# Opening of a hybrid encoder layer: first tokens loaded through two queues, and part of their normalization on ScalarE

## The chip, the cores and the metric

The kernel runs on one core of one Trainium2 chip. A core has five engines that work beside each other, each through its own list of instructions in order: TensorE (PE; PEld is its loading of stationary operands), VectorE (DVE), ScalarE (ACT), GpSimd (POOL) and SyncE (SP), which here only starts transfers (DMAs). Sixteen DMA engines move the data between the chip's memory and the core's SBUF. An engine waits for another through semaphores. The metric is the device time of one execution in microseconds (us); less is better.

## The reference, cut to what matters

```python
def layer_norm(x, g, b):
    mu = jnp.mean(xf, axis=-1, keepdims=True)
    var = jnp.mean(jnp.square(xf - mu), axis=-1, keepdims=True)
    return (xf - mu) * lax.rsqrt(var + LN_EPS) * g + b

def reference(x, emb_ln_g, emb_ln_b, w_in, conv_w, sink, w_out, ln_g, ln_b):
    h = layer_norm(x, emb_ln_g, emb_ln_b)          # x: 1 x 256 x 4096, float32
    p = h @ w_in[0]                                # 4096 x 13312
    ...                                            # gated convolution, windowed attention
    y = concat([y_conv, y_attn]) @ w_out[0]        # 4096 x 4096
    return layer_norm(2 ** 0.25 * h + y, ln_g[0], ln_b[0])
```

There are 256 tokens of 4096 features. Nearly all the work is in the two matrix products; the change lies wholly in the first `layer_norm` and in how its input comes in.

## The kernel before, in words

Every weight piece (128 x 2048 float32, 1 MB) is split into a high part in a rounded 32-bit format and the low remainder: ScalarE writes the high part (`split_hi`, L226, `whi`), VectorE the low one (`split_lo`, L230, `wlo`). Activations are split the same way into `xT` (`x_split`, L409 and L410). TensorE multiplies high by high, high by low and low by high (`mm`, L275; later in pairs of blocks at L300 to L303). The order of all engines is that of the code; no scheduler moves anything.

The opening deals with the 256 tokens in two halves of 128, `xs[0]` and `xs[1]`, with one token on each of 128 partitions. In turn:

- SP starts the transfers: `xs[0]` in six parts by columns (1024, 1024, 1024, 512, 256, 256), the scales `g_c` and `b_c`, the first weight piece `first[0]`, then `xs[1]` in four parts of 1024 columns with the halves of the weight piece `first[1]` between them, then the following weight pieces. Eight semaphores go round: each transfer waits until the one eight places earlier has landed.
- VectorE takes the statistics of `xs[0]` (`stats`, L354: nine instructions, seven over 512 columns and two over 256), combines them (`stats_end`, L357) and works out mean and 1/deviation in `musd` with one ScalarE instruction among four of its own (`small_chain`, L311 to L315; the ScalarE one is `y`). It then normalizes `xs[0]` in place in eight parts of 512 columns (`norm`, L362), takes the statistics of `xs[1]`, and normalizes that.
- TensorE first runs two matmuls without use, for warmth, as soon as columns 3072 to 3583 of `xs[0]` are there (L417). It turns the normalized parts (features onto partitions; `transp` L369 for parts 0 and 1, `transp2` L387 for the others), and ScalarE copies them out of PSUM into `hT` with the scale and bias of the layer norm (`turned1` L375, `turned2` L395).
- The products of the first two weight pieces are done in full float32 straight from `hT` (`first_mm`, L404): for the first tokens piece 0 and half of piece 1, then transposes of parts 2 and 3 of `xs[0]`, the rest of piece 1, and the same for the second tokens. From L275 on come the split weights, four rows of `hT` (a part) for each piece.

`musd[:, i, 2:3]` holds 1/deviation and `musd[:, i, 3:4]` holds minus mean times 1/deviation, so `x * musd[2] + musd[3]` is the normalized value too.

Of the kernel before, what the change touches and what calls it, by code (L numbers as in the profile page):

```python
# [8 lines left out]
F32 = mybir.dt.float32  # L9
F32R = mybir.dt.float32r  # L10
AF = mybir.ActivationFunctionType
# [3 lines left out]
P = 128  # L15
D = 4096
# [85 lines left out]
def encoder_kernel(ctx: ExitStack, tc: tile.TileContext, x, emb_g, emb_b, wi, ws, conv_w, sink, wo, ln_g, ln_b, out):  # L102
    nc = tc.nc
# [143 lines left out]
    musd = const.tile([P, 2, 4], F32, name="musd")  # L247
# [58 lines left out]
    def small_chain(i, dst):  # L306

        v = small.tile([P, 1], F32, name="v", bufs=1)
        y = small.tile([P, 1], F32, name="y0", bufs=1)
        t = small.tile([P, 1], F32, name="t", bufs=1)  # L310
        nc.scalar.activation(y, dst[:, i, 1:2], AF.Abs_reciprocal_sqrt, bias=eps_t)  # L311
        nc.vector.tensor_scalar(v, dst[:, i, 1:2], LN_EPS, -0.5, op0=ALU.add, op1=ALU.mult)
        nc.vector.scalar_tensor_tensor(t, y, v, y, op0=ALU.mult, op1=ALU.mult)
        nc.vector.scalar_tensor_tensor(dst[:, i, 2:3], t, 1.5, y, op0=ALU.add, op1=ALU.mult)
        nc.vector.scalar_tensor_tensor(dst[:, i, 3:4], dst[:, i, 0:1], -1.0, dst[:, i, 2:3], op0=ALU.mult, op1=ALU.mult)  # L315

    with tc.tile_pool(name="pro", bufs=1) as pro:
        warm = small.tile([P, 1], F32, name="sd", bufs=1)
        nc.scalar.activation(warm, eps_t, AF.Abs_reciprocal_sqrt)
        xs = [pro.tile([P, D], F32, name=f"x{i}") for i in range(2)]  # L320
        hT = pro.tile([P, KT, S], F32, name="hT")
        g_c = pro.tile([P, KT], F32, name="g_c")
        b_c = pro.tile([P, KT], F32, name="b_c")
# [1 line left out]
        def x_load(i, *cols):  # L325
            for c0, c1 in zip(cols, cols[1:]):
                nc.sync.dma_start(out=xs[i][:, c0:c1], in_=x[i * P:(i + 1) * P, c0:c1])
# [3 lines left out]
            nc.sync.dma_start(out=first[1][:, sl], in_=wi[IN_PIECES.index(steps[1][1:])][:, sl])  # L331

        first = [wpool.tile([P, PIECE + GAP], F32, name=f"first{j}", tag="whi")[:, OFF:OFF + PIECE] for j in range(2)]
        x_load(0, 0, 1024, 2048, 3072, 3584, 3840, 4096)
        nc.sync.dma_start(out=g_c, in_=emb_g)
        nc.sync.dma_start(out=b_c, in_=emb_b)
        load(0, first[0])
# [11 lines left out]
        NQ = KT // 4  # L349
# [6 lines left out]
        def stats_end(i):  # L356
            nc.vector.bn_aggr(musd[:, i, 0:2], st[i])  # L357
            small_chain(i, musd)

        def norm(i, q):  # L360
            sl = slice(q * 512, (q + 1) * 512)
            nc.vector.tensor_scalar(xs[i][:, sl], xs[i][:, sl], musd[:, i, 0:1], musd[:, i, 2:3],  # L362
                                    op0=ALU.subtract, op1=ALU.mult)

        def transp(i, q, pool, name):
            pt = pool.tile([P, 4, P], F32, name=name)
            for k in range(4):
                kt = q * 4 + k
                nc.tensor.transpose(pt[:, k, :], xs[i][:, kt * P:(kt + 1) * P], ident)  # L369
            return pt  # L370
# [30 lines left out]
        def first_mm(q, i, k0=0, k1=PK):  # L401
            for k in range(k0, k1):
                kt = q * PK + k
                nc.tensor.matmul(acc[0, i], hT[:, kt, i * P:(i + 1) * P], first[q][:, k * W:(k + 1) * W],  # L404
                                 start=(kt == 0), stop=False)
# [13 lines left out]
        for q in range(2):  # L419
            norm(0, q)  # L420
            t0.append(transp(0, q, ps_att, "att"))
# [1 line left out]
            turned1(0, q, t0[q])  # L423
        first_mm(0, 0)
        first_mm(1, 0, 0, 2)
        for q in range(2, NQ):
            norm(0, q)
        for c in range(NQ + 1):
            stats(1, c)
        transp2(2, (0,))  # L430
        transp2(3, (0,))
        first_mm(1, 0, 2, 4)
        stats_end(1)
        for q in range(NQ):
            norm(1, q)
        t1 = [transp(1, q, ps_acc, "acc") for q in range(2)]
# [398 lines left out]
    for j in range(n_pro, N_IN):  # L835
        kind, ci, q = steps[j]
# [332 lines left out]
```

## Time and profile before

| | |
|---|---|
| median of 3 runs | 1500.56 us (1500.46 to 1501.62) |
| the profiled execution | 1500.92 us, span 1499.2 us |
| TensorE busy | 1482.4 us (99%), granted clock 0.999 |
| VectorE busy | 1338.4 us (89%) |
| ScalarE busy | 803.3 us (54%) |
| DMA | 316.17 MB, mean 211 GB/s; 356 GB/s in the first 22 us |

All lines of the profile come from one execution. The span runs from its first instruction to its last, and the execution's own time is 1.7 us longer. Times in timelines count from the span's start. A row of a timeline gives the start, the length, the engine, the line of the code, the operation, its output and inputs, their shapes, how many instructions are merged in it, and in brackets how long the engine had been idle and what ended that. Buffers are named without their numbers: `x` is `xs[0]` or `xs[1]`, `first` is either of the first two weight pieces, `att` and `acc` are PSUM tiles, `st` the statistics.

### The profile page before, as it was taken

The numbers are of one execution on the slowest core, as the hardware profiler recorded it, in microseconds if no ns is written. First come the engines' busy times: TensorE is split into PE (matmuls) and PEld (weight loads), VectorE is DVE, ScalarE is ACT, GpSimd is POOL, SyncE is SP. The second block draws the span as 40 slices with busy tenths as digits, with TensorE's granted clock in tenths as the row PEclk, the third lists the DMA queues.
The fourth block names the chain that finished last, engine by engine and source line by source line (L and its number), as shares of the span: only waits on it lengthen the run. The fifth ranks groups of instructions, "written<-read, shape, count | busy, mean of one in ns | idle before, by whom it ended". The sixth has DMA issues, their size and how long they took to land.

```text
span 1499.2 us, 29810 instructions
## 1 busy us (share of the span) xinstructions
PE 1482.4 (99%) x12878; PEld 1465.4 (98%) x12878; DVE 1338.4 (89%) x1384; ACT 803.3 (54%) x687; POOL 1.3 (0%) x7
## 2 busy tenths in 40 slices
PE   7999999999999999999999999999999999999998
PEld 4999999999999999999999999999999999999997
DVE  7768999898999999999999999999998688888876
ACT  5544656766666665655555555555555444444431
POOL 0000000000000000000000000000000000000000
PEclk9999999999999999999999999999999999999999
DMA  8545465555554556646545655556558656756663
GB/s 318 217 183 196 164 217 189 192 197 208 180 204 176 190 201 209 230 177 224 200 182 219 231 198 197 225 204 241 191 207 313 233 201 220 290 215 230 219 237 113
DMA packets 71365, 316.17 MB, mean 211 GB/s; under 512 B 8545, under 2 KB 12609, under 8 KB 50113
## 3 DMA queue, kind: packets, MB, share of 16 engines
q1 hardware_dynamic: 70224, 312.43, 57.3%
q8 instruction: 101, 1.65, 0.4%
q10 hardware_dynamic: 1008, 1.84, 0.3%
q14 instruction: 32, 0.25, 0.0%
HBM read 305.23 MB, written 8.91 MB: 210 GB/s over the span
## 4 chain that ended last, share of the span: by engine, by line
PE 93%; DVE 3%; ACT 1%; issue 1%; DMA 1%; SPq 0%; ACTq 0%; DVEq 0%
PE acc L275 39%; PE acc L957 20%; PE pacc L301 6%; PE pacc L300 6%; PE pacc L303 6%; PE acc L301 4%; PE acc L300 4%; PE acc L303 4%; DVE wlo L230 1%; PE att L518 1%; ACT whi L226 1%; DVE st L354 0%; PE acc L404 0%; DMA wall<-in_ws 0%; DVE wall L192 0%
## 5 line engine op out<-in xcount | busy, mean ns | idle before, releaser
L226 ACT ACTIVATE whi<-wall 128x1792 fp32r<-128x1792 f32 (+1 forms) x284 | 501.7, 1772 | 464.6 <-DVE wall L194 149.7
L230 DVE TENSOR_TENSOR wlo<-wall,whi 128x1792 fp32r<-128x1792 f32 (+1 forms) x284 | 593.4, 2096 | 75.9 <-ACT whi L226 64.3
L275 PE MATMUL acc<-whi,xT 128*128 128x256 f32 x3584 | 427.6, 276 | 0.0
L275 PEld LDWEIGHTS acc<-whi,xT 128*128 128x128 f32 x3584 | 415.8, 188 | 0.0
L275 PE MATMUL acc<-wlo,xT 128*128 128x256 f32 x1792 | 221.3, 275 | 0.0
L275 PEld LDWEIGHTS acc<-wlo,xT 128*128 128x128 f32 x1792 | 211.4, 188 | 0.0
L226 ACT ACTIVATE whi<-w 128x2048 fp32r<-128x2048 f32 x73 | 140.7, 1927 | 114.6 <-PE acc L275 72.5
L957 PE MATMUL acc<-whi,xT 128*128 128x256 f32 x1696 | 201.8, 275 | 0.0
L957 PEld LDWEIGHTS acc<-whi,xT 128*128 128x128 f32 x1696 | 196.6, 188 | 0.4 <-issue 0.4
L230 DVE TENSOR_TENSOR wlo<-w,whi 128x2048 fp32r<-128x2048 f32 x73 | 166.8, 2286 | 10.8 <-ACT whi L226 10.6
L192 DVE TENSOR_TENSOR wall<-wall 128x1024 f32<-128x1024 f32 x93 | 113.3, 1218 | 11.0 <-DMA wall<-in_ws 8.7
L300 PE MATMUL acc<-whi,xT 128*128 128x256 f32 x416 | 114.7, 276 | 0.0
L301 PE MATMUL acc<-whi,xT 128*128 128x256 f32 x416 | 114.6, 276 | 0.0
L300 PE MATMUL pacc<-whi,xT 128*128 128x256 f32 x396 | 111.0, 280 | 0.0
L303 PE MATMUL pacc<-wlo,xT 128*128 128x256 f32 x396 | 109.2, 276 | 0.6 <-DVE wlo L230 0.4
L301 PE MATMUL pacc<-whi,xT 128*128 128x256 f32 x396 | 109.1, 276 | 0.0
L957 PE MATMUL acc<-wlo,xT 128*128 128x256 f32 x848 | 105.3, 275 | 0.0
L303 PE MATMUL acc<-wlo,xT 128*128 128x256 f32 x416 | 104.4, 275 | 0.0
L300 PE MATMUL pacc<-whi,SC 128*128 128x256 f32 x376 | 103.6, 275 | 0.0
L301 PE MATMUL pacc<-whi,SC 128*128 128x256 f32 x376 | 103.6, 275 | 0.0
L957 PEld LDWEIGHTS acc<-wlo,xT 128*128 128x128 f32 x848 | 100.4, 188 | 0.0
L303 PE MATMUL pacc<-wlo,SC 128*128 128x256 f32 x376 | 94.5, 276 | 0.0
(224 smaller groups left out, 1930.1 us busy)
## 6 DMA issues: line engine op xcount, KB each, us to landing
wall<-in_ws SPq DMA_DIRECT2D x202, 512.0 KB
w<-in_wi SPq DMA_DIRECT2D x73, 1024.0 KB
wall<-in_wo SPq DMA_DIRECT2D x43, 1024.0 KB
wall<-in_wi SPq DMA_DIRECT2D x39, 1024.0 KB
R<-in_wo SPq DMA_DIRECT2D x10, 1024.0 KB
x<-in_x SPq DMA_DIRECT2D x7, 512.0 KB
yl<-yd SPq DMA_DIRECT2D x7, 512.0 KB
xc<-in_x SPq DMA_DIRECT2D x14, 256.0 KB
```

Of the source, the lines that this page charges most:

```text
L192: nc.vector.tensor_tensor(t[:, :, 4:6, :], t[:, :, 1:3, :], t[:, :, 0:1, :].to_broadcast([P, 2, 2, HW]), op=ALU.add)
L226: nc.scalar.activation(part(j, wh[j]), part(j, raw[j]), AF.Copy)
L230: nc.vector.tensor_tensor(part(j, wl[j]), part(j, raw[j]), part(j, wh[j]).bitcast(F32), op=ALU.subtract)
L275: nc.tensor.matmul(acc[ci, i][:, c:c + HW], x, w[:, k * W + c:k * W + c + HW], start=(first and w is hi and k + off + c == 0), stop=(last ...
L300: nc.tensor.matmul(o, ah, hi[:, w, :], start=(opens and p == 0), stop=False)
L301: nc.tensor.matmul(o, al, hi[:, w, :], start=False, stop=False)
L303: nc.tensor.matmul(o, ah, lo[:, w, :], start=False, stop=(closes and last))
L518: nc.tensor.transpose(ps[:, c, i * P:(i + 1) * P], t[:, i, (2 * b + c) * P:(2 * b + c + 1) * P], ident)
L957: nc.tensor.matmul(acc[ci, i][:, c:c + HW], y, m[:, k * w + c:k * w + c + HW], start=(first and off + c == 0), stop=(last and c + HW == w))
```

## The change

The six transfers of `xs[0]` are written first. They are cut at other columns (512, 1024, 1024, 1024, 256, 256), and two of them, columns 0 to 511 and 1536 to 2559, are issued by ScalarE, ahead of its table load and its warming activation. Of the eight normalization parts of `xs[0]`, parts 0 and 1 stay on VectorE; parts 2 to 7 go to ScalarE as `Identity(scale * x + bias)` in the new `norm_act`. Parts 2 and 3 stand where all six stood; parts 4 to 7 stand behind the statistics of `xs[1]` (behind their `small_chain`) and ahead of the normalization of `xs[1]`.

```diff
     with tc.tile_pool(name="pro", bufs=1) as pro:
+        xs = [pro.tile([P, D], F32, name=f"x{i}") for i in range(2)]
+        for eng, c0, c1 in ((nc.scalar, 0, 512), (nc.sync, 512, 1536), (nc.scalar, 1536, 2560), (nc.sync, 2560, 3584),
+                            (nc.sync, 3584, 3840), (nc.sync, 3840, 4096)):
+            eng.dma_start(out=xs[0][:, c0:c1], in_=x[0:P, c0:c1])
         warm = small.tile([P, 1], F32, name="sd", bufs=1)
         nc.scalar.activation(warm, eps_t, AF.Abs_reciprocal_sqrt)
-        xs = [pro.tile([P, D], F32, name=f"x{i}") for i in range(2)]
...
-        x_load(0, 0, 1024, 2048, 3072, 3584, 3840, 4096)
...
+        def norm_act(q):
+            sl = slice(q * 512, (q + 1) * 512)
+            nc.scalar.activation(xs[0][:, sl], xs[0][:, sl], AF.Identity, scale=musd[:, 0, 2:3], bias=musd[:, 0, 3:4])
...
         first_mm(1, 0, 0, 2)
-        for q in range(2, NQ):
-            norm(0, q)
+        for q in range(2, 4):
+            norm_act(q)
         for c in range(NQ + 1):
             stats(1, c)
...
         stats_end(1)
+        for q in range(4, NQ):
+            norm_act(q)
         for q in range(NQ):
             norm(1, q)
```

What ScalarE has in its list from the start to the first split weight, before (`x_105` and `x_106` are the two halves of the tokens, `y_147` and `y_214` the ScalarE step of each half's statistics):

```order
L319 ACT_TABLE_LOAD
L319 ACTIVATE sd<-eps_t 128x1
L311 ACTIVATE y_147<-musd,eps_t 128x1
L375 ACTIVATE hT<-att,b_c,g_c 128x128 x8
L311 ACTIVATE y_214<-musd,eps_t 128x1
L375 ACTIVATE hT<-acc,b_c,g_c 128x128 x4
L226 ACTIVATE whi<-wall 128x2048
```

The same after the change (the first tokens are now `x_103`, the second step `y_210`; lines are a few numbers higher):

```order
L321 DMA x_103<-in_x 128x512
L321 DMA x_103<-in_x 128x1024
L323 ACT_TABLE_LOAD
L323 ACTIVATE sd<-eps_t 128x1
L311 ACTIVATE y_147<-musd,eps_t 128x1
L381 ACTIVATE hT<-att,b_c,g_c 128x128 x8
L369 ACTIVATE x_103<-x_103,musd 128x512 x2
L311 ACTIVATE y_210<-musd,eps_t 128x1
L369 ACTIVATE x_103<-x_103,musd 128x512 x4
L381 ACTIVATE hT<-acc,b_c,g_c 128x128 x4
L226 ACTIVATE whi<-wall 128x2048
```

Two transfers stand ahead of the table load, two parts ahead of the second `y`, and four between the second `y` and the first `hT` of the second tokens.

VectorE between the two statistics, before:

```order
L354 BN_STATS st_132<-x_105 128x6 x9
L357 BN_AGGR musd<-st_132 128x2
L312 TENSOR_SCALAR v<-musd 128x1
L313 SCALAR_TENSOR_TENSOR t<-y_147,v 128x1
L314 SCALAR_TENSOR_TENSOR musd<-t,y_147 128x1
L315 SCALAR_TENSOR_TENSOR musd<-musd 128x1
L362 TENSOR_SCALAR x_105<-x_105,musd 128x512 x8
L354 BN_STATS st_133<-x_106 128x6 x9
```

And after:

```order
L356 BN_STATS st_132<-x_103 128x6 x9
L359 BN_AGGR musd<-st_132 128x2
L312 TENSOR_SCALAR v<-musd 128x1
L313 SCALAR_TENSOR_TENSOR t<-y_147,v 128x1
L314 SCALAR_TENSOR_TENSOR musd<-t,y_147 128x1
L315 SCALAR_TENSOR_TENSOR musd<-musd 128x1
L364 TENSOR_SCALAR x_103<-x_103,musd 128x512 x2
L356 BN_STATS st_133<-x_104 128x6 x9
```

Only two normalizations are left between the statistics. SP's list loses two of the six transfers of the first tokens and is otherwise the same, and TensorE's list has the same instructions in the same order.

## The prediction

> **What bounds the kernel now.** I read the page's busy times first, then busy time by stretch, then the chain of waits and the four engines' timelines of the opening. The page and the stretches say where time can be lost at all (columns: stretch, its length, busy time of PE, PEld, DVE, ACT, POOL, then granted clock, DMA share, GB/s):
>
> ```profile
> span 1499.2 us, 29810 instructions
> PE 1482.4 (99%) x12878; PEld 1465.4 (98%) x12878; DVE 1338.4 (89%) x1384; ACT 803.3 (54%) x687; POOL 1.3 (0%) x7
> ...
> 0.00:22.00 22.00, 13.05 (x37) 6.14 (x38) 16.42 (x39) 4.97 (x12) 0.70 (x6) 1.00 0.94 356
> 22.00:1480.00 1458.00, 1454.97 (x12754) 1449.09 (x12754) 1310.02 (x1319) 795.53 (x669) 0.56 (x1) 1.00 0.58 209
> ```
>
> TensorE works 1482.4 of 1499.2 us. From 22 to 1480 us it idles 1458.00 - 1454.97 = 3.0 us; in the first 22 us, which the change edits, 9.0 us. What follows 22 us is one back-to-back stream of matmuls, so the change is worth what it moves the start of that stream, and nothing else unless a later link breaks. The chain of waits (start, length, what) shows who sets that start:
>
> ```profile
> 1.72 5.79 DMA x<-in_x
> ...
> 7.53 2.54 DVE st L354 x5
> ...
> 11.46 3.65 DVE x L362 x8
> 15.11 4.83 DVE st L354 x9
> ...
> 21.90 1.11 PE acc L369 x8
> ```
>
> So up to 21.90 the end hangs on the load of x and then on VectorE: statistics of the first 128 tokens, their eight normalizations, statistics of the second 128 tokens. The change takes six of those eight away. TensorE's own timeline, however, is nearly as tight (start, length, operation, count, idle before it and its releaser):
>
> ```profile
> 8.35 3.75 PE L417 MATMUL att<-x,ident 128*128 128x512 f32 x4 [8.35 <-DMA x<-in_x]
> 11.97 1.31 PE L369 MATMUL att<-ident,x 128*128 128x128 f32 x8
> 13.40 5.42 PE L404 MATMUL acc<-first,hT 128*128 128x512 f32 x12
> 18.65 1.04 PE L387 MATMUL att<-ident,x 128*128 128x128 f32 x8
> 19.53 1.88 PE L404 MATMUL acc<-first,hT 128*128 128x512 f32 x4
> 21.90 1.11 PE L369 MATMUL acc<-ident,x 128*128 128x128 f32 x8 [0.49 <-DVE x L362]
> 23.30 3.60 PE L404 MATMUL acc<-first,hT 128*128 128x512 f32 x8
> ```
>
> It is occupied from 11.97 to 19.53 + 1.88 = 21.41 without a listed idle time, then waits 0.49 us for VectorE. However much VectorE is relieved between the two statistics, at most 0.49 us can come of it unless the first tokens are ready sooner too.
>
> **Six normalizations leave VectorE.** Its timeline:
>
> ```profile
> 4.78 2.57 DVE L354 BATCH_NORM_STATS2 st<-x 128x6 f32<-128x512 f32 x4 [3.84 <-DMA x<-in_x]
> 7.53 2.53 DVE L354 BATCH_NORM_STATS2 st<-x 128x6 f32<-128x512 f32 x5 [0.18 <-DMA x<-in_x]
> 10.09 0.40 DVE L357 BATCH_NORM_AGGREGATE musd<-st 128x2 f32<-128x54 f32 x1
> ...
> 11.38 3.73 DVE L362 TENSOR_SCALAR x<-x,musd 128x512 f32<-128x512 f32 x8
> 15.02 4.90 DVE L354 BATCH_NORM_STATS2 st<-x 128x6 f32<-128x512 f32 x9
> 19.96 0.40 DVE L357 BATCH_NORM_AGGREGATE musd<-st 128x2 f32<-128x54 f32 x1
> ...
> 29.87 1.23 DVE L410 TENSOR_TENSOR xT<-hT,xT 128x1024 fp32r<-128x1024 f32 x1
> ```
>
> Eight parts take 3.73 us, so six free 6 x 0.466 = 2.8 us, and the second statistics could start at 12.3 instead of 15.02. But the data must be there. The SP queue tells when: each of its transfers waits for the one eight places earlier in the program to land, so a start after a wait is a landing time.
>
> ```profile
> 6.05 1.80 SPq L327 DMA_DIRECT2D x<-in_x  x2
> 8.23 0.33 SPq L331 DMA_DIRECT2D first<-in_wi  x1
> 8.60 0.90 SPq L327 DMA_DIRECT2D x<-in_x  x2
> ...
> 12.87 0.33 SPq L344 DMA_DIRECT2D cw<-in_conv_w  x1
> 14.16 0.33 SPq L345 DMA_DIRECT2D sk<-in_sink  x1
> 15.44 1.60 SPq L172 DMA_DIRECT2D wall<-in_wi  x2
> ```
>
> cw waits for columns 0 to 1023 of the second tokens (12.87), sk for 1024 to 2047 (14.16), the next weight piece for half of first[1] (15.44); the second of the pair at 15.44 starts at 15.44 + 1.60 - 0.33 = 16.7, when columns 2048 to 3071 are in. One quarter takes 1.28 us by these steps, so the last lands at about 18.0 (an estimate). Behind it stand one part of 512 columns and two of 256. Nine parts (seven of 512) took 4.90 us, the five at 7.53 (three of 512) 2.53, so one of 512 costs (4.90 - 2.53) / 4 = 0.59, the two of 256 together 2.53 - 3 x 0.59 = 0.76, and the three 1.35 us. With the usual step between two instructions the second aggregate starts at 19.4 instead of 19.96. **Gain on VectorE: 0.55 us, not 2.8**; the rest turns into waiting for the transfer.
>
> **The same six parts arrive on ScalarE.** Its timeline and the groups from which I price one (the number after the bar: busy, then mean ns of one):
>
> ```profile
> 10.53 0.29 ACT L311 ACTIVATE y<-musd,eps_t 128x1 f32<-128x1 f32 x1 [8.22 <-DVE musd L357]
> 12.89 2.90 ACT L375 ACTIVATE hT<-att,b_c,g_c 128x128 f32<-128x128 f32 x8 [2.07 <-PE att L369]
> 20.45 0.29 ACT L311 ACTIVATE y<-musd,eps_t 128x1 f32<-128x1 f32 x1 [4.66 <-DVE musd L357]
> 22.59 1.50 ACT L375 ACTIVATE hT<-acc,b_c,g_c 128x128 f32<-128x128 f32 x4 [1.85 <-PE acc L369]
> ...
> 27.15 3.79 ACT L395 ACTIVATE hT<-att,b_c,g_c 128x256 f32<-128x256 f32 x8
> ```
> ```profile
> L395 ACT ACTIVATE hT<-att,b_c,g_c 128x256 f32<-128x256 f32 x24 | 11.6, 601 | 6.5 <-PE att L387 6.5
> L587 ACT ACTIVATE th<-tab 128x512 f32<-128x512 f32 x16 | 9.9, 618 | 0.0
> L536 ACT ACTIVATE k<-acc 128x512 f32<-128x512 f32 x2 | 1.1, 588 | 0.0
> L702 ACT ACTIVATE q<-pacc 128x256 f32<-128x256 f32 x5 | 1.8, 364 | 0.0
> ```
>
> No row shows a 128x512 activation with a per-partition scale and bias. In a row, 128x128 ones with both cost 2.90 / 8 = 0.36 us and 128x256 ones 3.79 / 8 = 0.47; another 256 columns at that slope add 0.22, so 0.70 us a part. From below, the pair of plain 128x512 ones took 1.1 / 2 = 0.55; from above, 618 ns plus what the two operands cost at 256 columns (601 - 364 = 237) is 0.855. I take 0.70, which comes from the nearest form.
>
> Two parts (1.4 us) go behind the eight hT of the first tokens, at 15.8 to 17.2: inside the 4.66 us of idle time before the second y, and ahead of their reader, the transposes at 18.65. Cost nothing; without that idle time, up to 1.4 us. Four parts go behind the second y, and there the cover is short. Before, ScalarE idled 1.85 us between y (end 20.74) and the hT of the second tokens (22.59). After, y starts at 20.45 - 0.55 = 19.90 and ends at 20.19; four parts take 2.8 us, to 22.99. Queued behind them are the four hT, and behind these TensorE's first matmuls on the second tokens. The first hT takes 0.42 us (1.50 less three steps of 0.36), so it is ready at 23.41, and L404 starts at 23.45 to 23.5. Before it started at 23.30. TensorE could have been there sooner: its previous matmuls end at 21.41 plus whatever the first tokens lose, the first normalized part of the second tokens is ready 0.55 earlier (21.35), and 1.40 us of transposes (23.30 - 21.90) give 22.8 to 23.0. So the wait for VectorE goes, and a slightly longer one for ScalarE takes its place: **+0.2 us**.
>
> Farther on ScalarE runs 0.4 us later than before (22.99 against 22.59). Its next readers have room: the hi/lo split that the stream needs ended at 29.87 + 1.23 = 31.10, and the stream's third matmul, its first reader, came after 31.40; shifted by 0.4 and 0.2 it still fits. The four moved parts themselves are read only by transposes from 30.6 on.
>
> **First tokens through two queues.** Same bytes, six transfers as before, two of them issued by ScalarE. Below, the DMA engines in the microsecond from 3 us on, and a transfer that ScalarE issues near the end:
>
> ```profile
> 3.00:4.00 1.00, 0.00 (x0) 0.00 (x0) 0.00 (x0) 0.00 (x0) 0.00 (x0) 1.00 0.92 287
> ```
> ```profile
> 1493.93 0.34 ACTq L1003 DMA_DIRECT2D out<-R  x1
> ```
>
> An issue on ScalarE costs 0.34 us; two of them, ahead of the table load and the warming activation, are covered by the 8.22 us of idle time before the first y. Four x issues on SP instead of six bring nothing: the transfers behind them wait for landings anyway. The DMA engines are 0.92 busy with one queue, so I take the same bytes to land by the same time. Then the smaller first part (256 KB) lands near 4.1 instead of 4.78. But the end counts: columns 2560 to 3583 are now one transfer, complete when all columns below 3584 are, which is 8.23 (the issue that waited for it); behind it wait two parts of 512 and two of 256, which is one part less than after 7.53: 8.23 + 2.56 - 0.59 = 10.20 against 10.09. **About +0.1 us**, and 0.6 us if the two queues share evenly, since then columns 1536 to 2559 land only at 7.5 and six parts follow. TensorE's 21.41 becomes 21.5 to 22.0, transposes end by 23.4: still under ScalarE's 23.5. From below, a first part at 4.1 and nine parts in 4.90 us would end at 9.4 (the last 256 columns still land near 9.05, the second start of the pair at 8.60): -0.65 us. Even then the second tokens' path holds TensorE at 21.35.
>
> [...]
>
> **Rivals.** (1) Faster: activations overlap down to 0.55 us, four end at 22.39 and hT is ready at 22.81; TensorE, 0.1 us late on the first tokens, comes at 22.9: -0.4 us, 1500.15. For it speaks that 601 ns rows follow each other every 474; against it, 0.55 is the price without operands. (2) Slower: the DMA engines serve SP's queue first. SP holds 1.3 MB of x, so ScalarE's columns 1536 to 2559 would come last, at about 9.05, with six parts behind: 9.05 + 2.56 + 0.59 = 12.2, 2.1 us late. TensorE's 21.41 becomes 23.5 and its lead of 0.49 is gone: +1.6 us, 1502.2. It decides once the first statistics end over 0.7 us late. No row shows two loading queues at once. (3) The change does not do its main thing: the second tokens land 0.5 us later or the statistics wait otherwise, y stays at 20.45, hT at 20.74 + 2.8 + 0.42 = 23.96: +0.7 us, 1501.3.
>
> **How the numbers follow.** The profiled execution took 1500.92 us (span 1499.2 and 1.7 around it), the median run 1500.56; +0.2 makes 1501.1 of the first and 1500.8 of the second, which is what I predict. Chances: the sum as reckoned (-0.1 to +0.6) 0.50, faster 0.27, SP first 0.11, no gain on VectorE 0.08, something unseen later in the stream 0.04. The shifts reach from -0.45 to +1.65; the three runs spread over 1.2 us, 0.6 each way, so 1499.5 to 1502.6 would hold them all, and I cut the upper end to 1502.4. A measurement tells 0.2%, 3.0 us, from no change; every case named stays under that, as the whole idle time of the opening is 9 us and most of it stands before data can be there. Faster by more 0.02, slower by more 0.03, within 0.95.
>
> **What would show it.** In the profile after: the second statistics in pieces with idle times released by x, ending near 19.4; ScalarE without idle time between the second y and the hT; L404 on the second tokens released by ScalarE near 23.5; the first aggregate near 10.2. I am wrong if that L404 starts before 23.0 or after 24.0, if an activation part takes under 0.6 or over 0.8 us in a row, or if idle time of TensorE between 22 and 1480 us leaves 3 us by more than one.

## The result, and the profile after

The changed kernel takes 1503.55 us in the median of 21 runs (1502.83 to 1505.0), the kernel before 1500.78 us (21 runs, 1499.89 to 1502.34): 2.8 us slower, a ratio of 1.002 with a 95% interval of 1.0013 to 1.0026. The forecast was +0.2 us, with a range that ended at 1502.4. The profiled execution took 1503.52 us, of which 1501.8 are the span.

Page and stretches of the changed kernel (columns as before):

```profile
span 1501.8 us, 29812 instructions
PE 1483.3 (99%) x12878; PEld 1466.3 (98%) x12878; DVE 1336.2 (89%) x1378; ACT 807.6 (54%) x693; POOL 1.3 (0%) x7
...
0.00:22.00 22.00, 12.07 (x29) 5.94 (x30) 13.31 (x32) 6.99 (x15) 0.70 (x6) 1.00 0.92 352
22.00:1480.00 1458.00, 1455.29 (x12752) 1448.92 (x12751) 1310.89 (x1321) 797.59 (x672) 0.56 (x1) 1.00 0.58 209
```

The long stream is as dense as before: 1458.00 - 1455.29 = 2.7 us idle, against 3.0. The loss lies at the two ends. Timelines of VectorE and SP in the opening (the code's lines are 2 to 6 higher than before):

```profile
5.56 1.88 DVE L356 BATCH_NORM_STATS2 st<-x 128x6 f32<-128x512 f32 x3 [4.62 <-DMA x<-in_x]
8.64 3.12 DVE L356 BATCH_NORM_STATS2 st<-x 128x6 f32<-128x512 f32 x6 [1.20 <-DMA x<-in_x]
11.80 0.40 DVE L359 BATCH_NORM_AGGREGATE musd<-st 128x2 f32<-128x54 f32 x1
...
17.93 2.64 DVE L356 BATCH_NORM_STATS2 st<-x 128x6 f32<-128x512 f32 x5 [1.22 <-DMA x<-in_x]
20.60 0.40 DVE L359 BATCH_NORM_AGGREGATE musd<-st 128x2 f32<-128x54 f32 x1
```
```profile
5.55 0.33 SPq L172 DMA_DIRECT2D first<-in_wi  x1
```

The smaller first part did not come sooner: first[0], which waits for it, is issued at 5.55, and the first statistics start at 5.56 (4.78 before). Three follow each other, then VectorE waits 1.20 us for columns 1536 to 2559, until 8.64. Six instructions are left there, where before five were left at 7.53, and the first aggregate comes at 11.80 instead of 10.09. TensorE:

```profile
8.33 3.75 PE L423 MATMUL att<-x,ident 128*128 128x512 f32 x4 [8.33 <-DMA x<-in_x]
13.68 1.97 PE L375 MATMUL att<-ident,x 128*128 128x128 f32 x8 [1.60 <-DVE x L364]
15.44 6.22 PE L410 MATMUL acc<-first,hT 128*128 128x512 f32 x12
21.50 1.04 PE L393 MATMUL att<-ident,x 128*128 128x128 f32 x8
22.37 1.88 PE L410 MATMUL acc<-first,hT 128*128 128x512 f32 x4
24.09 1.04 PE L375 MATMUL acc<-ident,x 128*128 128x128 f32 x8
...
25.40 3.60 PE L410 MATMUL acc<-first,hT 128*128 128x512 f32 x8
```

The useless matmuls start as early as before (8.33; columns 2560 to 3583 are in). Behind them, however, TensorE now idles 1.60 us, and what follows is slow: the same eight transposes take 1.97 us instead of 1.31, the next twelve records 6.22 instead of 5.42. From the transposes to the rest of first[1] (22.37 against 19.53) the delay grows from 1.71 to 2.84 us. It then shrinks, since TensorE no longer waits for VectorE (24.09 against 21.90, +2.2; 25.40 against 23.30, +2.1). That +2.1 enters the stream, as the chain of waits of both kernels shows at the same matmuls, before and after:

```profile
31.65 5.50 PE acc L275 x48
```
```profile
33.74 5.50 PE acc L275 x48
```

Of it the stream gives 0.5 us back, for the last matmul comes at 1495.80 against 1494.25; then the end costs another 1.1. The waits of SP's queue at the end, before and after (engine, line, waited for; us in total, times, longest):

```profile
SPq L1164 <- DMA out<-R: 3.3, 1, 3.3
```
```profile
SPq L1172 <- DMA out<-R: 4.4, 1, 4.4
```

So in these two executions the 2.6 us of span are 2.1 - 0.5 + 1.1, rounded.

### The profile page after: what moved, and what is told of

It reads as the page before. It is cut to its first block, busy times and chain, and to the rows that moved or that the text cites. A ratio compares the mean times of both kernels' runs of the same rounds, so it can differ in the third digit from the quotient of the medians.

```text
span 1501.8 us, 29812 instructions
## 1 busy us (share of the span) xinstructions
PE 1483.3 (99%) x12878; PEld 1466.3 (98%) x12878; DVE 1336.2 (89%) x1378; ACT 807.6 (54%) x693; POOL 1.3 (0%) x7
## 3 DMA queue, kind: packets, MB, share of 16 engines
q10 hardware_dynamic: 1296, 2.62, 0.5%
q8 instruction: 101, 1.65, 0.4%
## 4 chain that ended last, share of the span: by engine, by line
PE 91%; DVE 5%; ACT 2%; DMA 1%; issue 1%; ACTq 0%; DVEq 0%
PE acc L275 37%; PE acc L965 20%; PE pacc L301 6%; PE pacc L300 6%; PE pacc L303 6%; PE acc L301 4%; PE acc L300 4%; PE acc L303 4%; DVE wlo L230 2%; PE acc L410 1%; PE att L526 1%; ACT whi L226 1%; DMA wall<-in_ws 1%; DVE wall L192 1%; DMA x<-in_x 0%
```

## The experiments

Times are medians; the kernel before ran beside each: 1501.32, 1501.31 and 1501.28 us in the three groups with timed runs. Where the 95% interval of a ratio takes in 1, the time alone does not show a difference. The times of the links, from the profiles' timelines (us; "second" is for the second tokens). The last row is from the trace's records of the granted clock, each of which says when a grant begins and how long it holds. Ahead of the first record the clock column of the views prints 1.00, but TensorE is slow there: four useless 128x512 records took 3.75 us in the kernel before, ahead of its first record, and 1.88 us in two kernels below whose record begins earlier.

| | before | changed | loads only | normalizations only | late aggregate |
|---|---|---|---|---|---|
| first aggregate | 10.09 | 11.80 | 11.73 | 10.19 | 12.04 |
| first transposes, start and length | 11.97, 1.31 | 13.68, 1.97 | 13.61, 1.97 | 12.08, 1.46 | 13.93, 1.11 |
| rest of first[1], first tokens | 19.53 | 22.37 | 23.62 | 19.78 | 22.96 |
| second transposes | 21.90 | 24.09 | 25.34 | 21.50 | 24.68 |
| second products | 23.30 | 25.40 | 26.65 | 23.51 | 25.99 |
| full clock from | 12.48 | 17.19 | 19.79 | 12.88 | 12.02, but half from 15.43 to 18.84 |

**Loads only.** The changed loads with the normalizations of before.

```diff
-        for q in range(2, 4):
-            norm_act(q)
+        for q in range(2, NQ):
+            norm(0, q)
...
-        for q in range(4, NQ):
-            norm_act(q)
```

> Only the loads of the first tokens as changed (two queues, new cuts); all eight normalizations on VectorE as before. Theory (the two queues do the harm: ScalarE's columns 1536 to 2559 land near 8.6, the first aggregate comes near 11.8 instead of 10.1, TensorE idles 1.6 us ahead of its first transposes and runs them and the next matmuls at half speed): all of that is seen again, stream start (third step, first L275) 2 to 4 us later than before, time 2 to 4 us above the kernel before; more than the changed kernel, if VectorE's six parts now hold up the second statistics. Rival (the normalizations on ScalarE do the harm): aggregate near 10.1, time within 0.5 us of before.

1503.62 us, ratio 1.0015 (1.0006 to 1.0023), 2.3 above before.

```profile
13.61 1.97 PE L375 MATMUL att<-ident,x 128*128 128x128 f32 x8 [1.58 <-DVE x L364]
15.37 7.55 PE L410 MATMUL acc<-first,hT 128*128 128x512 f32 x12
```

The late aggregate, the idle time and the slow transposes are all there without any work moved to ScalarE. That it would lose more than the changed kernel does not show in the median. In its profile it does (second products at 26.65 against 25.40), because there the full clock began only at 19.79, so that TensorE worked slowly from 13.61 on for over 6 us (eight transposes in 1.97 us, 1.04 at full clock; twelve records of the first products in 7.55, 5.42 before); that execution was the slowest of its eleven.

**Normalizations only.** The changed normalizations with the loads of before.

```diff
-        for eng, c0, c1 in ((nc.scalar, 0, 512), (nc.sync, 512, 1536), ...
-            eng.dma_start(out=xs[0][:, c0:c1], in_=x[0:P, c0:c1])
+        x_load(0, 0, 1024, 2048, 3072, 3584, 3840, 4096)
```

> Only the normalizations as changed (six parts on ScalarE); the loads as before, all on SP. Theory: the first aggregate at 10.1, no idle time of TensorE beyond 0.1 us before its first transposes; second aggregate near 19.4; first products of the second tokens at 23.4 to 23.5 held by ScalarE, time +0.2 us against before (-0.3 to +0.6). Rival (ScalarE's parts do the harm): 2 us or more above before.

1501.78 us, +0.5 (ratio 1.0003, 0.9994 to 1.0012). Its ScalarE, and its first products of the second tokens:

```profile
20.00 0.30 ACT L311 ACTIVATE y<-musd,eps_t 128x1 f32<-128x1 f32 x1 [2.55 <-DVE musd L357]
20.20 2.92 ACT L367 ACTIVATE x<-x,musd 128x512 f32<-128x512 f32 x4
23.02 1.47 ACT L379 ACTIVATE hT<-acc,b_c,g_c 128x128 f32<-128x128 f32 x4
...
23.51 3.70 PE L408 MATMUL acc<-first,hT 128*128 128x512 f32 x8 [0.50 <-ACT hT L379]
```

Four parts take 23.02 - 20.20 = 2.82 us, 0.70 each, with no idle time around them, and TensorE waits 0.50 us for what stands behind them. The second aggregate is at 19.50. This half of the forecast holds link by link.

**The new cuts on one queue.**

```diff
-        for eng, c0, c1 in ((nc.scalar, 0, 512), ..., (nc.scalar, 1536, 2560), ...
+        for eng, c0, c1 in ((nc.sync, 0, 512), ..., (nc.sync, 1536, 2560), ...
```

> The changed kernel with all six transfers of the first tokens on SP: same cuts, one queue. Theory (the second queue does the harm, not the cuts): columns 2560 to 3583 land near 8.2, first aggregate near 10.2, time within 0.6 us of before. Rival (the cuts do it): aggregate at 11 or later, time 1.5 us or more above before.

1501.60 us, +0.3 (ratio 1.0003, 0.9994 to 1.0012), but its profile (an execution of 1503.09 us) had the aggregate at 11.52. Three more profiles were taken:

> The changed kernel with all six transfers of the first tokens on SP, profiled once more, since the first profile's execution was the slowest of its eleven. Theory (in that one two of the 16 DMA engines landed 0.9 and 1.3 us after the others, by chance): here columns 2560 to 3583 land at 8.2 to 8.5, aggregate at 10.2 to 10.5. Rival (these cuts are always that late): aggregate at 11.5 again.

> The changed kernel with all six transfers of the first tokens on SP, a third profile. Theory (the late landings of the first two profiles are chance: single DMA engines that come 0.4 to 1.3 us after the rest): columns 2560 to 3583 at 8.2 to 8.6, aggregate at 10.2 to 10.6. Rival (small first transfer on one queue makes DMA engines straggle): aggregate at 11 or later again.

> The same, a fourth profile, with the same two expectations: aggregate at 10.2 to 10.6 by chance alone in the others, at 11 or later if these cuts make DMA engines straggle.

These single executions took 1503.84, 1501.68 and 1501.52 us (one of the kernel before beside the last two 1500.71), with the aggregate at 11.21, 11.16 and 11.06. The last:

```profile
4.29 0.69 DVE L356 BATCH_NORM_STATS2 st<-x 128x6 f32<-128x512 f32 x1 [3.35 <-DMA x<-in_x]
5.56 1.29 DVE L356 BATCH_NORM_STATS2 st<-x 128x6 f32<-128x512 f32 x2 [0.58 <-DMA x<-in_x]
7.76 3.26 DVE L356 BATCH_NORM_STATS2 st<-x 128x6 f32<-128x512 f32 x6 [0.91 <-DMA x<-in_x]
...
9.20 3.40 PE L423 MATMUL att<-x,ident 128*128 128x512 f32 x4 [9.20 <-DMA x<-in_x]
```

That it was chance is refuted: the parts land in the written order, the first at 4.29, but columns 1536 to 2559 come at 7.76 and 2560 to 3583 at 9.20. In all four profiles the latter come at 9.20 to 9.66, at least 0.6 us later than the 8.2 to 8.6 that I had reckoned. On one queue these cuts thus cost the aggregate 1.0 to 1.4 us. The useless matmuls are late with the last of these parts and run up to the transposes (idle there 0.34 us at most), so little of that becomes idle time of TensorE. The lateness itself does reach the second products, which start at 24.42 to 26.32 in these profiles (the last with 1.4 us of waiting for the first weight pieces in it); the timed runs, with +0.3 us and an interval from 0.9 below to 1.8 above, do not say how much of it holds in every execution. In the trace's landings of columns 2560 to 3583 the 16 DMA engines are 1.8 to 1.9 us apart (0.8 in the fourth part before), with about the same middle. Why these cuts spread them was not found.

**Only the first part on ScalarE's queue.**

```diff
-        (nc.scalar, 1536, 2560), (nc.sync, 2560, 3584),
+        (nc.sync, 1536, 2560), (nc.sync, 2560, 3584),
```

> The changed kernel with columns 1536 to 2559 given back to SP, so that only columns 0 to 511 come through ScalarE's queue, beside SP's 512 to 1535. Theory (two queues are served in turn row by row, so transfers in flight together land together): first statistics at 5.3 to 5.7 and not at 4.1, three in a row, then columns 1536 to 2559 alone at 6.8 to 7.2, first aggregate near 10.3, time 0.2 to 1.0 us above before. Rival (served transfer by transfer): first statistics near 4.1, with a wait before the second. Second rival (ScalarE's queue is served last): first statistics after 6.

1501.66 us, +0.4 (ratio 1.0003, 0.9994 to 1.0012).

```profile
5.51 4.91 DVE L356 BATCH_NORM_STATS2 st<-x 128x6 f32<-128x512 f32 x9 [4.58 <-DMA x<-in_x]
10.46 0.40 DVE L359 BATCH_NORM_AGGREGATE musd<-st 128x2 f32<-128x54 f32 x1
```

The first part (256 KB), beside SP's 512 KB in flight at the same time, is there at 5.51, not at 4.1, and all nine statistics then run without a wait. The trace shows why: a transfer is 128 rows, and from 3.5 to 4.5 us the DMA engines start 62 rows of 2 KB from ScalarE's queue and 58 of 4 KB from SP's. The rows of the two queues are taken about in turn here, although those of the one are twice as long, and the two transfers end together (last landings 5.30 and 5.49). In the changed kernel the first pair does the same (67 rows of 2 KB and 66 of 4 KB start from 3.5 to 4.5 us, last landings 5.54 and 5.31), and so does the pair of 1024 columns: 49 rows from ScalarE's queue and 50 from SP's start from 5.5 to 6.5 us, and columns 2560 to 3583 are in at 8.19 and columns 1536 to 2559 at 8.62. With one pair the aggregate is 0.4 us late, with the second pair 1.7. The cuts are the same in both kernels, so the difference of 1.3 us is that of the queue.

**A late aggregate, nothing else.** The kernel before with three statistics done twice.

```diff
+        for c in range(3):
+            stats(0, c)
         stats_end(0)
```

> The kernel before with three statistics instructions over 512 columns done twice ahead of the aggregate (results unchanged), so that the first aggregate comes 1.8 us later, at 11.9, with no load and no normalization moved. Theory (a late aggregate costs its own lateness and, by TensorE's idle time ahead of the transposes, some 1.1 us at half clock, less the 0.5 us that TensorE waited for VectorE): stream start 2.2 to 2.9 us later, time 2.2 to 2.9 above before, the transposes 1.9 us long. Rival (only the lateness counts): 1.3 to 1.8 us.

1503.57 us, ratio 1.0014 (1.0005 to 1.0024), +2.3. The interval, 0.8 to 3.6 us, takes in the rival's times too, so the profile has to decide. The lateness was 1.95 us, the second products came 2.7 later: more than the lateness less the 0.49 us of slack, 1.5. Here the profile shows the clock at work (a row of TensorE's timeline, then stretches: length, busy time of PE, granted clock, DMA share, GB/s):

```profile
13.93 1.11 PE L369 MATMUL att<-ident,x 128*128 128x128 f32 x8 [1.72 <-DVE x L362]
```
```profile
12.50:15.00 2.50, 1.07 (x8) 1.00 1.02 418
15.50:18.80 3.30, 3.30 (x5) 0.50 1.04 422
19.00:21.00 2.00, 2.00 (x6) 1.00 1.02 422
```

TensorE idles 1.72 us ahead of its transposes, runs them still at full clock (1.11 us, not the 1.9 expected), and is then granted half the clock from 15.43 to 18.84. Here it falls into the first products, whose twelve records take 7.11 us instead of 5.42. In the changed kernel a like idle time costs something else: the full clock, which began at 12.48 before, has not begun when the transposes start at 13.68, and comes at 17.19. Counted back from there in stretches of 3.41 us (the length of both grants here; that the stretches run on ahead of the first record is my estimate), the idle time lies in the one from 10.36 to 13.78, which TensorE would otherwise have worked through.

**The changed kernel kept busy.** 24 matmuls of the identity from the start on, four useless matmuls instead of two.

```diff
-        for _ in range(2):
+        for _ in range(24):
+            nc.tensor.matmul(wu[:, 0:P], ident, ident, start=True, stop=True)
+        for _ in range(4):
             nc.tensor.matmul(wu, ident, xs[0][:, 3072:3584], start=True, stop=True)
```

> The changed kernel with more matmuls without use ahead of the first transposes: 24 of the identity from 1.5 us on and four instead of two on columns 3072 to 3583, so that TensorE has no long idle time before 13.6. Theory (half of the loss is TensorE's clock, not granted in full until 17.5 because of the idle time at 12.1 to 13.7): the first aggregate still near 11.8, but the eight transposes take 0.9 to 1.0 us instead of 1.97 and the first products have 0.43 us steps from the start; 0.7 to 1.2 us faster than the changed kernel, 1.4 to 2 us above before, and less scatter between runs. Rival (the clock has nothing to do with it, the first transposes are slow because of something they wait for): they take 1.9 us again and the time is that of the changed kernel.

1502.84 us, ratio 1.001 (1.0001 to 1.0019), 1.5 above before. The changed kernel was 2.8 above the kernel before, so some 1.2 us are gone, more or less the error of both. Less scatter was expected; the runs lie between 1501.65 and 1503.88, which is no less.

```profile
13.60 1.11 PE L375 MATMUL att<-ident,x 128*128 128x128 f32 x8 [1.32 <-DVE x L364]
14.80 5.42 PE L410 MATMUL acc<-first,hT 128*128 128x512 f32 x12
...
24.87 2.84 PE L410 MATMUL acc<-first,hT 128*128 128x512 f32 x6 [0.49 <-ACT hT L381]
```

The aggregate is as late as in the changed kernel (11.72), but the full clock begins at 5.19, 3.75 us after the first matmul at 1.44, and the transposes and first products run at full speed from the start. The delay no longer grows behind the transposes: 1.63 us there, 1.40 at the rest of first[1]. Then ScalarE's four parts hold TensorE for 0.49 us, as they did with the old loads. With full clock the forecast wait appears.

**Both profiled again.**

> The changed kernel profiled once more. Theory: the two 1024-column transfers that share the engines land 0.5 us apart or less near 8.2 to 8.6 again and the first aggregate comes at 11.5 to 12.0 again; the last output lands about 2 us after its issue, not 3.1 as in the first profile, where one of 16 DMA engines was 1.15 us late. Rival: the late end belongs to the change.

One execution, 1504.47 us. Aggregate at 11.59, transposes 1.97 us long, full clock from 17.66: the opening repeats. The late end repeats too: SP waited 4.5 us for the last output, of whose 16 DMA engines one landed 1.2 us behind the others, as in the first profile (1.15). That it was chance was the expectation, and it is not borne out; with more useless matmuls the wait was 3.9, with either half of the change alone 3.3, as before, and 3.3 too with columns 1536 to 2559 given back to SP. What ties it to the whole change was not found.

> The kernel before, profiled once more, to see whether the moment at which the full clock is granted moves between executions: theory, anywhere from 12.1 to 15.5 us; rival, 12.5 again.

One execution, 1502.07 us. TensorE's transposes take 1.11 us in this profile of the kernel before, 1.31 in the first, and 1.46 and 1.58 in two kernels (normalizations only, and the next one) whose opening up to there is the same. The full clock begins at 11.92, 12.48, 12.88 and 13.10 in them: the grant does move between executions.

**One part behind y instead of four.** Loads as before, parts 2 to 6 ahead of the second y (the edit is shown against the normalizations of the changed kernel).

```diff
-        for q in range(2, 4):
+        for q in range(2, 7):
             norm_act(q)
...
-        for q in range(4, NQ):
-            norm_act(q)
+        norm_act(7)
```

> Loads as before, normalization parts 2 to 6 on ScalarE ahead of the second y (in its 2.55 us of idle time), only part 7 behind it. Theory (four parts behind y made ScalarE the last link in the kernel with only the normalizations changed): no wait for ScalarE ahead of the first products of the second tokens, these at 22.8 to 23.0 against 23.31 before and 23.52 there; time 0.3 to 0.5 us below before, 0.6 below the kernel with four behind. Rival (VectorE's or TensorE's own path sets the end): products at 23.3 to 23.5, time as before.

1500.77 us, 0.5 below before (ratio 0.9998, 0.9989 to 1.0006). No wait for ScalarE is left:

```profile
20.73 0.80 ACT L367 ACTIVATE x<-x,musd 128x512 f32<-128x512 f32 x1
22.68 1.51 ACT L379 ACTIVATE hT<-acc,b_c,g_c 128x128 f32<-128x128 f32 x4 [1.14 <-PE acc L373]
...
23.39 3.60 PE L408 MATMUL acc<-first,hT 128*128 128x512 f32 x8
```

The products start at 23.39, not at 22.8 to 23.0 but where the rival had them. In this execution x landed later (second aggregate at 20.04, 19.50 with the normalizations only), and TensorE's own path was late as well: it was free for the second transposes only at 21.93 and started them at 21.98. So earlier data would have brought 0.05 us here.

**More useless matmuls, without the changed loads.** The kernel with one part behind y, and the kernel before, each with

```diff
+        for _ in range(24):
+            nc.tensor.matmul(wu[:, 0:P], ident, ident, start=True, stop=True)
```

> The same with 24 matmuls of the identity from 1.5 us on, ahead of the two without use. Theory (TensorE's full clock is granted one stretch of 3.4 us or more after it starts to work without a gap, at a moment that varies from run to run; before, that falls between 12.1 and 15.5): granted by 8 us in every run, transposes in 1.1 us; 0.2 us faster than the version without in the profile and 0.5 to 1.0 in the median. Rival (the grant comes at a fixed time): within 0.3 us of the version without.

> The kernel before with 24 matmuls of the identity from 1.5 us on, and nothing else. Theory (in the kernel before the full clock is granted at 12 to 15.5, when the first transposes are already due): median 0.3 to 0.8 us below before and less scatter; products of the second tokens at 23.0 to 23.4, since VectorE's path to 21.9 stays. Rival (VectorE's path alone sets the start of the stream): within 0.2 us of before.

1500.07 us (1499.79 to 1501.15; ratio 0.9993, 0.9984 to 1.0002) and 1500.28 us (1499.91 to 1500.80; ratio 0.9994, 0.9985 to 1.0003). Medians 1.2 and 1.0 us below before, with intervals that just take in 1; the second's eleven runs lie within 0.9 us, where the 21 of before beside it spread over 1.85. The full clock begins at 5.29 and 5.87. Useless matmuls on x, transposes and second products of the first, transposes and second products of the second:

```profile
8.72 1.88 PE L423 MATMUL att<-x,ident 128*128 128x512 f32 x4
12.30 1.11 PE L373 MATMUL att<-ident,x 128*128 128x128 f32 x8 [1.70 <-DVE x L362]
...
22.97 3.60 PE L408 MATMUL acc<-first,hT 128*128 128x512 f32 x8
```
```profile
12.11 1.12 PE L369 MATMUL att<-ident,x 128*128 128x128 f32 x8 [1.23 <-DVE x L362]
...
23.45 3.60 PE L404 MATMUL acc<-first,hT 128*128 128x512 f32 x8
```

The first of the two is the lowest median of all kernels tried, but its profiled execution is no faster than the one without (1500.01 against 1499.89 us; 0.2 less was expected). In the second the second products start at 23.45, no earlier than the 23.30 of before. So where the lower medians come from is not shown by these profiles.

## Why the prediction was wrong

**First tokens.** This step failed. It said that the same bytes land by the same time and that the aggregate would be 0.1, at most 0.6 us later. The bytes did land almost by the same time (columns 2560 to 3583 by 8.33, when TensorE starts on them; after 8.64 VectorE never waits for x again in that half), but the two transfers of 1024 columns in flight on two queues were taken about row by row in turn (49 and 50 rows from 5.5 to 6.5 us) and ended together (8.62 and 8.19), so VectorE got late the 1024 columns that it needed early: the aggregate came 1.71 us late. The even share by bytes, the worst case inside the sum, was too mild: columns 1536 to 2559 came at 8.62, not at 7.5. The rival in which ScalarE's columns come last had 0.11 and priced the aggregate at 2.1 late. That this is near the 1.71 is luck, since they landed with columns 2560 to 3583 and not last, and its 1502.2 still falls short of 1503.55. The 0.1 for the new cuts was wrong on one queue as well, where they cost the aggregate 1.0 to 1.4 us.

**TensorE behind a late aggregate.** This term was missing from the sum and from every rival. I priced lateness one to one. After the idle time between the useless matmuls and the transposes TensorE was slow, in the changed kernel until the full clock began at 17.19 (eight transposes in 1.97 us, 1.04 at full clock), in the late kernel while the half clock recorded from 15.43 to 18.84 held: 2.84 - 1.71 = 1.1 us, with the late aggregate alone 3.43 - 1.96 = 1.5, with the loads alone 4.09 - 1.64 = 2.45. The profile before had the sign of it, and I read past it: a transpose group of 1.31 us where eight of the same kind took 1.04 at 18.65, and four useless 128x512 records in 3.75 us where twelve of that form took 5.42. The 1.00 of the clock column in the first 22 us hid it, as no grant was on record before 12.48.

**The end.** A last output that lands 1.1 us later, in both profiles of the changed kernel, was not foreseen and is not explained.

**What held.** VectorE's gain: 19.50 for the second aggregate with the old loads, 19.4 forecast. A part on ScalarE: 0.70 us, as forecast. ScalarE as the last link, with the old loads: products at 23.51, 23.45 to 23.5 forecast. The stream's later links did not break. In the changed kernel ScalarE's wait did not show because TensorE came later still, at 24.09 + 1.3; with full clock it did.

**The sum.** The second products start at 25.40, past the 24.0 that I had named as the sign of being wrong. The delay at the stream is 2.1 us: 1.71 by the loads and 1.13 by the clock, less 0.74 that the chain gives back (2.84 - 2.10; 0.49 of it is the wait for VectorE). The forecast was 0.2. By the runs the loads with what follows are worth 2.3 us (loads only), the normalizations 0.5, which is within their error. The range was given 0.95; its upper end also adds up to 1502.8 (1500.56 + 1.65 + 0.6), not to the 1502.6 written there, and 1503.55 lies above either.

## What to carry to other kernels

Before a load is split over two queues, ask which piece is needed first: here pieces of 128 rows each, in flight on two queues, arrived together (last landings 5.54 and 5.31, then 8.62 and 8.19), and with the DMA engines 0.92 busy or more from 3 to 12 us already before, the split postponed the first statistics from 4.78 to 5.56. Price a delay ahead of TensorE with the clock too: gaps of 1.5 to 1.7 us cost themselves and 1.1 us or more behind them where the full clock had not begun (17.19 to 19.79 in three profiles) or only just (12.02); where it began by 6 us (5.19 to 5.87), gaps of 1.2 to 1.7 us cost no more than themselves. Matmuls without use from the start on took some 1.2 us off the changed kernel, and with the old loads 0.7 and 1.0 us off the median; none of this is clear of the error. Work moved to an idle engine goes into the idle time, not behind the instruction that ends it: by the waits in the profiles, five of six parts ahead of y cost nothing, and four behind it held the next stage.

## What the runs showed of the hardware

In the late kernel the trace records full clock for TensorE from 12.02 to 15.43, half to 18.84, then full: two grants of 3.41 us. The one long grant of full clock holds for 1484.80 us in the profile of the kernel before and for 1481.38 in that of the changed kernel, also 3.41 apart. The full clock first came at 12.48 and at 11.92 in two profiles of the kernel before, at 17.19 and 17.66 in two of the changed one, and at 5.19 to 5.87 in the three kernels with 24 more matmuls without use. From TensorE's first matmul, or the first behind the gap where there is one ahead of the grant, that is 4.1 us (8.35 to 12.48) and 3.3 (8.63 to 11.92) in the kernel before, 3.5 (13.68 to 17.19) in the changed one and 6.2 (13.61 to 19.79) with the loads only.

Behind an idle time of 1.72 us came work and then the half clock in the late kernel (half from 15.43, twelve records in 7.11 us); behind one of 1.32 us the full clock stayed in the changed kernel kept busy (1.11 and 5.42 us), and so it did behind one of 1.70 in the best kernel (1.11 and 5.42). If stretches of 3.41 us are counted from each recorded grant, which is my estimate and in no record, the 1.72 us lie within one stretch (12.02 to 15.43), the 1.70 across the end of one (12.11). TensorE was then busy 0.47 of the stretch ahead of the half clock, and 0.59 (changed kernel kept busy) and 0.56 (best kernel) of those with the gaps that kept the full clock. Ahead of the first grant it was busy 0.21 of one stretch and all of the next in the kernel before (5.65 to 9.06, 9.06 to 12.48), 0.53 and all in the changed one (10.36 to 13.78, 13.78 to 17.19). These shares are estimates from the timelines, as the ends of matmuls are modelled.

Two loads in flight on the queues of SP and ScalarE were taken about row by row in turn: with only the first part on ScalarE's queue, 62 rows of the one and 58 of the other in one microsecond, and last landings 0.2 us apart although one load had half the bytes. In the changed kernel the same pair gave 67 and 66 rows and last landings 5.54 and 5.31. The page of the profile counts every row as a packet: ScalarE's queue has 1296 packets in the changed kernel and 1008 before, 288 more for two loads of 128 rows, each with 16 packets of 4 bytes besides.
